# An encoder layer on one core: which queue issues the stores

## The chip, the cores and the metric

The kernel runs on one core of a Trainium2 chip. The metric is the time of one execution on the device in microseconds, without the host's work. Its engines each take their own instructions in the order in which they are written: TensorE (PE in the profile, PEld its weight loads), VectorE (DVE), ScalarE (ACT), GpSimd (POOL) and SyncE (SP). A DMA is issued by one of these queues: an issuing instruction waits until what it reads or overwrites is ready, and whatever stands behind it on the same queue waits too. The data is then moved by 16 DMA engines that all queues share.

## The reference

An encoder layer, applied to a sample of 1024 positions and to a prompt of 512, with the same weights and a width of 2048:

```
h = rms_norm(x, norm_g)
c_val, c_glu, c_gate, q, k, v, a_gate = split(h @ w_in)        # 2048 -> 5632, 44 blocks of 128
q, k = apply_rope(q), apply_rope(k)                            # 8 query heads, 2 key heads of 128
conv = silu(layer_norm(depthwise_conv31(c_val * sigmoid(c_glu)))) @ w_pw * silu(c_gate)
attn = banded_sink_attention(q, k, v, sink) * silu(a_gate)     # within 128 positions
y = rms_norm(x + concat(conv, attn) @ w_out, final_norm_g)
```

Everything is float32. The kernel splits each float32 operand of a large product into a high part, rounded for TensorE, and the low rest, and takes three products (high-high, high-low, low-high).

## The kernel before, in words

The positions lie along the free axis and 128 channels along the partitions. The sample comes first. Its input projection is cut into units of two column blocks and eight row blocks: a `Unit` computes a 2 by 2 block product with seven block products instead of eight (`P1` to `P7`), some 19 us on TensorE for each unit. It runs over the conv columns first (first half of the rows, then the second), then over gate, key, value, query and attention-gate columns. The first half's results are partial sums: `finish` (line 240) stores them into DRAM tiles named `part_...`. In the second half `finish` calls `add_into` (line 428), a DMA on GpSimd's queue that adds the stored part into the tile in SBUF; four or five products later the unit's `done` step works on the tile on VectorE and ScalarE and stores the result in DRAM (`gate_d`, `ag_d`, `h_d`, `q_d`, `k_d`, `v_d`).

For queries and keys the `done` step is `rotate` (line 947): `rope` (lines 928 to 933) makes two products on VectorE, and `put_rotated` (line 941) stores one of them and then adds the two halves of the other into the same DRAM rows with two `add_into` calls, which have to wait until the store has landed:

```
e.store(dst, o)
e.add_into(dst[0:half], b[half:])
e.add_into(dst[half:], b[0:half])
```

Behind the units come the prompt's projection, by whole columns (`Job`), then the pointwise product of the convolution, the output product of the sample (units again, with `y_d` and lines 1219 to 1239), and last the prompt's pointwise and output products (`last_run`). The convolution's taps run on VectorE beside all of these (line 906), fed from `h_d` and stored in `conv_d`; attention runs between the products of the prompt's jobs and reads `q_d`, `k_d`, `v_d` back and stores `att_d`. Weight blocks are loaded by SP into one of three `raw` buffers (lines 117 to 123, 332) and split by ScalarE and VectorE into one of three `hl` buffers (`parts`, lines 438 and 439). The low parts are stored once (`low_...`) and loaded for the prompt.

Tiles that are evicted from PSUM by line 217 come from two rings of four buffers, `g` and `u`; a buffer is free again when the store from it has landed. The products of `rotate` use a ring of four `a` buffers.

The order of work is written out by the program with lanes that give VectorE and ScalarE work between the products; then the tile framework puts each engine's instructions in an order by priorities and its own estimate of durations, and adds the waits.

Nearly all plain stores go through one helper, `store` (line 431). Accumulating DMAs go through `add_into`. The last rows of the prompt's output are stored by line 1531, which calls SP itself. All loads call SP themselves.

Of the kernel before, what the change touches and what calls it, by code (L numbers as in the profile page):

```python
# [358 lines left out]
class Encoder:  # L359
# [69 lines left out]
        self.nc.gpsimd.dma_start(dst, src, accum_op=ALU.add)  # L429

    def store(self, dst, src):
        self.nc.sync.dma_start(dst, src)

    def parts(self, hi, lo, x, g=None):

# [1421 lines left out]
```

## Time and profile before

| | |
|---|---|
| median of 3 runs | 2138.23 us |
| lowest and highest | 2134.34, 2139.43 us |
| span of the profiled execution | 2137.4 us |
| median against that span | 0.8 us more |
| TensorE busy | 2085.0 us, 98% |
| VectorE busy | 1668.7 us, 78% |
| ScalarE busy | 1063.8 us, 50% |
| GpSimd busy | 156.6 us, 7% |
| data moved by DMA | 473.04 MB, 221 GB/s on average |

The profile is of one execution. A line such as `L439 DVE ... hl<-raw,hl` names the line of the kernel, the engine, and what is written from what by the program's tile names. For a wait, the name behind `<-` is the instruction or DMA that ended it, as far as the semaphores tell; a wait for several things is put down to the last. Issuing a DMA isn't counted as busy time on SP, and it is on GpSimd.

### The profile page before, as it was taken

The numbers are of one execution on the slowest core, as the hardware profiler recorded it, in microseconds if no ns is written. First come the engines' busy times: TensorE is split into PE (matmuls) and PEld (weight loads), VectorE is DVE, ScalarE is ACT, GpSimd is POOL, SyncE is SP. The second block draws the span as 40 slices with busy tenths as digits, with TensorE's granted clock in tenths as the row PEclk, the third lists the DMA queues.
The fourth block names the chain that finished last, engine by engine and source line by source line (L and its number), as shares of the span: only waits on it lengthen the run. The fifth ranks groups of instructions, "written<-read, shape, count | busy, mean of one in ns | idle before, by whom it ended". The sixth has DMA issues, their size and how long they took to land. (4 is left out here: it accounts for less than half of the span.)

```text
span 2137.4 us, 26915 instructions
## 1 busy us (share of the span) xinstructions
PE 2085.0 (98%) x9330; PEld 1711.9 (80%) x9330; DVE 1668.7 (78%) x2551; ACT 1063.8 (50%) x1736; POOL 156.6 (7%) x184
## 2 busy tenths in 40 slices
PE   8999999999999999899999999999999989999998
PEld 7878888888888787688888888878888867887886
DVE  8757899988898788888887786668799667887543
ACT  7475436333554344554556776235545464563232
POOL 0001110000013233001000000000000001110000
PEclk9999999999999999999999999999999999999999
DMA  8888878854768888966664546886766369799952
GB/s 288 306 286 246 229 178 266 279 179 157 232 179 184 198 178 222 279 176 174 168 213 161 197 158 227 317 298 232 256 237 206 107 209 267 188 299 314 306 177 79
DMA packets 241209, 473.04 MB, mean 221 GB/s; under 512 B 23088, under 2 KB 80816, under 8 KB 241072
## 3 DMA queue, kind: packets, MB, share of 16 engines
q1 hardware_dynamic: 218992, 431.99, 60.5%
q0 software_dynamic: 22080, 39.33, 11.6%
q8 instruction: 73, 1.20, 0.2%
q14 instruction: 64, 0.52, 0.1%
HBM read 319.19 MB, written 152.04 MB: 220 GB/s over the span
## 5 line engine op out<-in xcount | busy, mean ns | idle before, releaser
L191 PE MATMUL a<-t,hl 128*128 128x512 f32 x2640 | 636.6, 392 | 22.5 <-ACT u L217 12.3
L191 PEld LDWEIGHTS a<-t,hl 128*128 128x128 f32 x2640 | 495.5, 189 | 132.8 <-ACT u L217 16.4
L438 ACT ACTIVATE hl<-raw 128x1024 fp32r<-128x1024 f32 (+1 forms) x330 | 296.2, 898 | 376.9 <-DVE raw L138 82.8
L439 DVE TENSOR_TENSOR hl<-raw,hl 128x1024 fp32r<-128x1024 f32 (+1 forms) x330 | 338.4, 1026 | 182.3 <-ACT hl L438 180.4
L906 DVE SCALAR_TENSOR_TENSOR f<-f,c_w_dw,f 128x1024 f32<-128x1024 f32 (+1 forms) x464 | 456.5, 1014 | 0.0
L578 PE MATMUL a<-t,hl 128*128 128x512 f32 x1344 | 328.9, 394 | 2.2 <-DVE f L848 2.2
L191 PE MATMUL c<-t,hl 128*128 128x512 f32 x1320 | 320.1, 390 | 1.6 <-ACT g L217 0.9
L578 PEld LDWEIGHTS a<-t,hl 128*128 128x128 f32 x1344 | 249.1, 188 | 53.0 <-DVE f L848 2.6
L191 PEld LDWEIGHTS c<-t,hl 128*128 128x128 f32 x1320 | 247.6, 188 | 53.8 <-ACT g L217 1.5
L578 PE MATMUL c<-t,hl 128*128 128x512 f32 x672 | 168.1, 397 | 0.0
L578 PE MATMUL b<-t,hl 128*128 128x512 f32 x672 | 162.6, 392 | 0.8 <-DVE hl L439 0.8
L191 PE MATMUL b<-t,hl 128*128 128x512 f32 x660 | 161.1, 390 | 0.0
L578 PEld LDWEIGHTS b<-t,hl 128*128 128x128 f32 x672 | 125.2, 188 | 26.1 <-DVE hl L439 1.2
L578 PEld LDWEIGHTS c<-t,hl 128*128 128x128 f32 x672 | 124.8, 189 | 24.4
L191 PEld LDWEIGHTS b<-t,hl 128*128 128x128 f32 x660 | 123.5, 188 | 25.1
L217 ACT ACTIVATE u<-a 128x512 f32<-128x512 f32 x114 | 67.2, 592 | 75.4 <-PE a L191 64.0
L217 ACT ACTIVATE g<-a 128x512 f32<-128x512 f32 x106 | 62.8, 592 | 76.8 <-PE a L191 70.3
L1540 PE MATMUL a<-hl,t 128*128 128x512 f32 x192 | 74.3, 390 | 0.0
L346 ACT ACTIVATE hl<-raw 128x1024 fp32r<-128x1024 f32 x44 | 46.4, 1054 | 46.7 <-PE b L578 15.2
L429 POOL DMA_DIRECT2D u<-part_out x16 | 14.0, 890 | 756.5 <-DVE t L439 697.4
L1044 ACT ACTIVATE p<-p,tiny 128x384 f32<-128x384 f32 (+1 forms) x96 | 54.5, 569 | 29.6 <-DVE tiny L1041 21.1
L438 ACT ACTIVATE a<-pt 128x512 fp32r<-128x512 f32 x64 | 38.0, 594 | 59.4 <-PE pt L1064 59.3
(312 smaller groups left out, 2581.2 us busy)
## 6 DMA issues: line engine op xcount, KB each, us to landing
raw<-w_in SPq DMA_DIRECT2D x171, 512.0 KB, 5.3
raw<-w_out SPq DMA_DIRECT2D x64, 256.0 KB, 4.5
raw<-w_out SPq DMA_DIRECT2D x31, 512.0 KB, 4.6
raw<-w_pw SPq DMA_DIRECT2D x24, 512.0 KB, 5.1
p<-xT_s SPq DMA_DIRECT2D x40, 256.0 KB, 5.3
f<-x_s SPq DMA_DIRECT2D x16, 512.0 KB, 7.2
f<-y_d SPq DMA_DIRECT2D x16, 512.0 KB, 5.9
y_s<-f SPq DMA_DIRECT2D x16, 512.0 KB, 4.6
```

Source lines behind the costliest of these rows:

```text
L191: nc.tensor.matmul(acc, hl[:, l, o, j, :], toks[j][:, r], start=name in FRESH and j == 0 and q == 0, stop=name in LAST and j == HALF - 1 a ...
L217: nc.scalar.activation(t, bank, AF.Copy)
L346: e.nc.scalar.activation(t[:, 0], raw, AF.Copy)
L429: self.nc.gpsimd.dma_start(dst, src, accum_op=ALU.add)
L438: nc.scalar.activation(hi, x, AF.Copy)
L439: nc.vector.tensor_tensor(lo, x, hi.bitcast(F32), ALU.subtract)
L578: nc.tensor.matmul(job.acc[0], hl[:, l, kk // HALF, kk % HALF, :], r, start=i == 0 and p == 0, stop=i == nk - 1 and p == 2,)
L906: nc.vector.scalar_tensor_tensor(t, h[:, j : j + T], w(j), t, ALU.mult, ALU.add)
L1044: nc.scalar.activation(p[:, 0:n], p[:, 0:n], AF.Exp, bias=nm[:, h : h + 1], accum_out=l[:, h : h + 1])
L1540: nc.tensor.matmul(acc, self.mix[self.KS[i]][:, m, b * P : (b + 1) * P], part[l].rearrange("p a b -> p (a b)"), start=i == 0 and p == 0, s ...
```

## The change

The helper `store` issues its DMA on GpSimd's queue and no longer on SP's. Nothing else in the program changes: `add_into`, the loads, and the prompt's last rows (line 1531) keep their queues.

```
     def add_into(self, dst, src):
         self.nc.gpsimd.dma_start(dst, src, accum_op=ALU.add)
 
     def store(self, dst, src):
-        self.nc.sync.dma_start(dst, src)
+        self.nc.gpsimd.dma_start(dst, src)
```

More of the change, by code (lines that the diff above doesn't have):

```diff
@@ L431, in store @@
     def store(self, dst, src):
-        self.nc.sync.dma_start(dst, src)
+        self.nc.gpsimd.dma_start(dst, src)
     def parts(self, hi, lo, x, g=None):
```

## The prediction

> **What bounds the kernel now.** I read the page first, then the busy time of each engine by stage, then who TensorE and VectorE wait for in the stage where GpSimd is used most, then the two DMA queues.
>
> ```profile
> span 2137.4 us, 26915 instructions
> PE 2085.0 (98%) x9330; PEld 1711.9 (80%) x9330; DVE 1668.7 (78%) x2551; ACT 1063.8 (50%) x1736; POOL 156.6 (7%) x184
> ```
>
> TensorE is busy 2085.0 of 2137.4 us, so all that any change can win is 52.4 us, and what a change can lose is whatever new waiting it forces on TensorE. SP and GpSimd matter only through that. By stage (busy us of each engine, clock, DMA share, GB/s):
>
> ```profile
> core 0: us, PE busy (x) PEld busy (x) DVE busy (x) ACT busy (x) POOL busy (x), PEclk, DMA share, GB/s
> ...
> 640.00:850.00 210.00, 203.04 (x895) 165.75 (x894) 168.02 (x226) 84.36 (x131) 69.08 (x80) 1.00 0.84 195
> 850.00:905.00 55.00, 44.68 (x188) 34.86 (x187) 44.16 (x65) 30.74 (x47) 8.45 (x10) 0.94 0.96 287
> 905.00:1400.00 495.00, 494.99 (x2308) 406.63 (x2307) 386.73 (x639) 275.68 (x466) 15.11 (x18) 1.00 0.64 200
> ...
> 1750.00:1910.00 160.00, 152.63 (x662) 123.81 (x661) 137.94 (x212) 95.38 (x154) 27.87 (x32) 0.99 0.88 244
> ```
>
> From 905 to 1400 us TensorE never stops. The place to look at is 640 to 850 us, where the ten key and query units of the sample sequence end: TensorE loses 7.0 us there, VectorE is idle for 210.0 - 168.0 = 42.0 us, and GpSimd issues 80 transfers. Who TensorE, and then VectorE, waits for in that window (us in total, times, longest):
>
> ```profile
> PE a L191 <- ACT u L217: 4.4, 3, 2.4
> PE a L191 <- DVE hl L439: 1.3, 1, 1.3
> PE a L191 <- ACT g L217: 1.2, 2, 0.7
> ```
>
> ```profile
> DVE a L932 <- issue: 17.8, 5, 8.0
> DVE a L932 <- DMA g<-part_kv: 7.1, 2, 6.7
> ...
> DVE u L882 <- DMA u<-part_gate: 3.2, 1, 3.2
> DVE a L932 <- DMA u<-part_q: 2.8, 2, 2.4
> DVE g L882 <- DMA g<-part_q: 2.4, 4, 1.2
> DVE a L932 <- DMA g<-part_q: 1.8, 1, 1.8
> DVE u L882 <- DMA u<-part_q: 1.7, 3, 0.7
> ```
>
> These seven groups hold 18 waits and 36.8 us, nearly all of VectorE's 42.0 us of idle time. Six name an accumulating DMA of line 429 (`add_into`, already on GpSimd's queue): the partial product is added into the tile and lines 932 and 882 need the sum. For the first the releaser isn't shown; line 932 needs the same sum and a free `a` tile, which another add of GpSimd's frees, so I count it in. VectorE takes its instructions in order, so a late add holds up the weight preparation of line 439 and, through ScalarE, TensorE.
>
> Why those adds are late is seen on the queues. Instructions of GpSimd, SP and VectorE from 740 to 750 us (start, us, what, idle before):
>
> ```profile
> 740.07 0.90 POOL L429 DMA_DIRECT2D g<-part_q  x1 [1.79 <-DVE g L237]
> 749.03 1.69 POOL L429 DMA_DIRECT2D q_d<-a  x2 [8.06 <-DVE a L932]
> 750.16 2.38 POOL L429 DMA_DIRECT2D u<-part_q  x2
> ```
>
> ```profile
> 742.23 0.32 SPq L432 DMA_DIRECT2D q_d<-u  x1
> ...
> 749.90 0.32 SPq L432 DMA_DIRECT2D q_d<-g  x1
> ```
>
> ```profile
> 747.97 0.69 DVE L932 TENSOR_TENSOR a<-g,f 128x512 f32<-128x512 f32 x1 [1.79 <-DMA g<-part_q]
> ```
>
> `put_rotated` stores the query (742.23, on SP) and then adds two halves into the same DRAM rows (749.03, on GpSimd). The adds must wait until the store has landed. GpSimd stands still for 8.06 us, and the next partial sums (750.16) stand behind.
>
> **The change part by part.** Every call of `store` moves: 464 issues (line 432's groups added up). The loads stay on SP, and the 16 stores of line 1531 too. Durations (ns, minimum/median/maximum) and landing times (us) of line 432 and of line 429, and who waits for a store:
>
> ```profile
> L432 SPq DMA_DIRECT2D att_d<-u x24: 525/561/922, 920.2 to 1733.5; - x24
> ...
> L432 SPq DMA_DIRECT2D q_d<-g x16: 319/320/566, 711.1 to 1048.4; - x16
> ...
> who waited for it (us, times):
>   POOL q_d L429: 75.4, 9
> ...
> DMA to landing us min/median/max: 2.0/3.8/11.7
> ```
>
> ```profile
> L429 POOL DMA_DIRECT2D q_d<-a x32: 821/848/1942, 693.1 to 849.5; - x32
> L429 POOL DMA_DIRECT2D u<-part_conv x16: 862/868/1005, 180.3 to 322.0; - x16
> ...
> DMA to landing us min/median/max: 2.8/6.0/11.9
> ```
>
> *Issue.* A store of 128 rows takes SP 320 ns; the nearest row on GpSimd, an add of 128 rows, takes 868 ns: 0.548 us more. GpSimd's busy time goes to 156.6 + 464 x 0.868 = 559 us, 26% of the span, so its sum is no bound; the order in it can be.
>
> *The rotated units (640 to 850 us).* Each add now has at least one store's issue ahead of it that ran beside it on SP. I charge each of the 18 VectorE waits 0.548 us: 9.9 us, and let all of it reach the end, since VectorE's idle time there is already made of such waits. The bounds: low, only the share of these waits that TensorE feels now (4.4 + 1.3 + 1.2 = 6.9 of 36.8, 0.19), 1.9 us; high, the store also lands later by the difference of the two medians, 6.0 - 3.8 = 2.2 us, so 18 x 2.75 = 49.5 us. I take 9.9, nearer the low end: the longer landing is that of an add, which reads what it adds to, and a store doesn't.
>
> *The queue behind.* A store waits for its data on GpSimd now, and adds and other stores wait behind it. Who holds SP in the same window (us, times, longest):
>
> ```profile
> SPq L123 <- DVE hl L439: 51.3, 10, 5.6
> SPq L432 <- DVE u L933: 44.9, 10, 9.4
> SPq L432 <- DVE g L933: 43.0, 10, 8.5
> ...
> SPq L1709 <- DMA q_d<-a: 9.5, 1, 9.5
> ```
>
> SP stands 87.9 us before the query stores, with gate stores and weight loads behind; this leaves SP, and is not new on GpSimd, which waits for the landing of those same stores anyway. What SP gains is loads that go out earlier. But its longest other wait (line 123) is for a buffer that VectorE frees, and stays.
>
> *Transition (850 to 905 us).* The one long stall of TensorE:
>
> ```profile
> PE a L191 <- ACT u L217: 5.3, 1, 5.3
> ```
>
> ScalarE is late because loads of the second sequence's rows (line 1709) wait for an `a` tile, freed by a query add (the 9.5 us above). The add stands behind a query store, so the store's later issue moves this by +0.5 us; bounds -5.3 (the load's cause gone) and +2.75.
>
> *Output units (1750 to 1910 us).* 32 stores into `y_d` join 32 adds. Each add can have one more issue ahead: at most 32 x 0.548 = 17.5 us for VectorE, which is idle 160.0 - 137.9 = 22.1 us there; I take 0. Without that cover it is +17.5; it could be a gain of all that TensorE loses there, 7.4 us.
>
> *Attention and the second sequence (905 to 1400 us).* The `att_d` stores have four pieces per row and take SP 561 ns. GpSimd's price lies between 868 ns (no more than for one piece) and 4 x 868 = 3472 ns; I take the lower end, since 64 rows cost 848 ns and 128 rows 868, so the count of pieces hardly shows. GpSimd is busy 15.1 of 495 us there and TensorE waits for nothing: 0. If one such store stood before a query add each time, 24 x 3.47 = 83 us would fall on a queue with 480 us free.
>
> *Freed loads.* What TensorE waits for after 905 us through ScalarE's preparation of loaded data:
>
> ```profile
> PE s L1030 <- ACT a L438: 3.5, 1, 3.5
> ...
> PE a L191 <- ACT hl L438: 2.3, 1, 2.3
> ...
> PE pt L191 <- ACT hl L438: 1.4, 1, 1.4
> ```
>
> Together 7.2 us. If stores no longer stand before those loads, between 0 and 7.2 us comes back. I take a third, -2.4 us: SP's loads also wait for one another's buffers.
>
> *Sum:* 9.9 + 0.5 + 0 + 0 - 2.4 = +8.0 us. The profiled span of 2137.4 becomes 2145.4; the median of the runs, 2138.2, stands 0.8 us above that span, so the forecast is 2146.2, slower by 0.37%. About 0.3% (6.4 us) is what a measurement of this kernel can tell from no change.
>
> A rule speaks against the change: the Trainium skill, SBUF — State Buffer, "SBUF: two separate sides", says that GpSimd, which builds its own descriptors, is shut out while VectorE runs in a two-port mode, so a transfer from GpSimd's queue can wait out VectorE's work. The trace bears little of it out: with VectorE busy most of each stage, the 16 adds of 180 to 322 us stay within 862 to 1005 ns. By the row the sum stays +8.0; by the rule it would be the fourth rival below.
>
> **The rivals.** *Faster.* SP no longer stands 87.9 us before query stores, gate stores free their tiles without passing weight loads, and adds aren't later because GpSimd was only waiting. Then some of the 7.0 us of 640 to 850, the 5.3 us at the transition and the 7.2 us of loads goes: 19.5 us, half of it gives 2128.5. It decides from the point where the store's later issue hides inside the 8.06 us. Against it: TensorE's waits name evictions and weights behind VectorE, not loads.
>
> *No difference.* VectorE's waits shift without growing, as TensorE feels only 0.19 of them: 18 x 0.548 x 0.19 + 0.5 - 2.4 = 0.0 us, so 2138.2. For it: TensorE's 98%.
>
> *GpSimd becomes the bound of the rotated units.* A unit takes 210/10 = 21.0 us. It has 8 adds (80 by ten) and now 4 stores: 12 x 0.868 = 10.4 us of issuing. Two landings of a query store are waited for; if both take 8.06 us with nothing else allowed past, the unit takes 26.5 us, 5.5 more, ten times: 55 us, 2193. It decides from a wait of (21.0 - 10.4)/2 = 5.3 us each, which lies between the medians 3.8 and 6.0. Against it: two stores' landings can overlap.
>
> *Starved issues.* VectorE's work holds up GpSimd's issues: all as long as the longest seen, 1942 ns. A rotated unit takes 12 x 1.942 + 8.06 = 31.4 us, 10.4 more, ten times: 104 us, 2242. Against it: the medians 848 and 868.
>
> That the stores don't move, or move without a new order on the engines, isn't a case I can price: the framework plans each engine's order anew, and a few us either way may come from that alone.
>
> **How the numbers follow.** Forecast 0.36, with a range of its own of 2141 to 2156; no difference 0.30; faster 0.22; GpSimd the bound 0.10; starved 0.02. The forecast's low end lies inside 0.3%, so 0.03 of it goes to "same": faster 0.22, same 0.33, slower 0.45. The range: 2127 takes in the faster case's middle and leaves 0.08 below; 2174 reaches two thirds of the way to the third rival's 2193 and leaves 0.10 above, starved issues among it.
>
> **What would show it.** Right: line 432 under GpSimd with some 868 ns each; VectorE's waits at lines 932 and 882 from 640 to 850 us above 36.8 us by about 10; the busy time of TensorE unchanged and its idle time there up from 7.0 to about 17 us; the stage 905 to 1400 still full. Wrong: waits at 932 and 882 that stay or shrink (no difference, or faster), SP's waits for line 933 gone and TensorE's idle time after 850 us smaller (faster), GpSimd busy or waiting for all of the stage and the units at 24 us or more (the bound), issues well over 1 us while VectorE runs (starved). A loss in a stage that I priced at 0, above all 905 to 1400 us or 1750 to 1910 us, would make the prediction wrong even if the total fits.

## The result, and the profile after

| | before | after |
|---|---|---|
| median (4 runs each, side by side) | 2138.83 us | 2164.01 us |
| lowest and highest | 2134.34, 2141.11 us | 2161.74, 2165.36 us |
| ratio, 95% interval | | 1.011 [1.0093, 1.0126] |
| span of the profiled execution | 2137.4 us | 2163.3 us |

The change makes the kernel about 25 us slower. The two profiled executions differ by 25.9 us, and TensorE alone accounts for it. The page of the kernel after, its span and the busy time of each engine:

```profile
span 2163.3 us, 27145 instructions
PE 2096.7 (97%) x9330; PEld 1719.8 (79%) x9330; DVE 1666.9 (77%) x2551; ACT 1062.4 (49%) x1736; POOL 416.2 (19%) x648
```

The same 9330 matmuls kept TensorE busy for 2096.7 us instead of 2085.0: +11.7 us for the same work, which is a matter of the clock. Its idle time went from 2137.4 - 2085.0 = 52.4 to 2163.3 - 2096.7 = 66.6 us: +14.2. The two add up to 25.9. VectorE and ScalarE did the same work in the same time. GpSimd's busy time rose by 259.6 us to 19% of the span, so that sum isn't the bound.

Where the idle time lies is seen by stage. First the stages of the kernel before that the prediction didn't show, then those of the kernel after (us from the start; length, then busy us of each engine, clock, DMA share, GB/s):

```profile
0.00:160.00 160.00, 150.06 (x646) 122.53 (x647) 113.26 (x186) 100.25 (x163) 0.20 (x4) 1.00 0.85 294
...
1400.00:1560.00 160.00, 156.50 (x714) 129.85 (x713) 124.31 (x212) 84.33 (x143) 0.00 (x0) 0.99 0.74 252
1560.00:1750.00 190.00, 186.69 (x853) 152.65 (x852) 147.50 (x256) 96.45 (x179) 0.00 (x0) 1.00 0.55 186
...
1910.00:2137.00 227.00, 216.40 (x960) 178.38 (x958) 120.25 (x202) 68.65 (x109) 0.00 (x0) 0.99 0.70 227
```

```profile
0.00:160.00 160.00, 149.52 (x638) 121.73 (x639) 110.98 (x183) 98.18 (x160) 33.32 (x65) 0.99 0.82 290
...
640.00:850.00 210.00, 202.08 (x889) 165.99 (x888) 167.56 (x223) 84.72 (x130) 94.47 (x124) 0.99 0.84 191
850.00:905.00 55.00, 45.11 (x183) 35.74 (x181) 41.68 (x55) 31.61 (x46) 13.00 (x18) 0.91 0.97 299
905.00:1400.00 495.00, 488.45 (x2265) 400.16 (x2265) 392.58 (x653) 274.88 (x469) 64.90 (x101) 0.99 0.65 207
1400.00:1560.00 160.00, 159.47 (x733) 132.23 (x732) 113.05 (x190) 77.84 (x124) 15.74 (x28) 1.00 0.68 227
1560.00:1750.00 190.00, 182.51 (x833) 149.02 (x832) 146.84 (x262) 92.94 (x181) 30.28 (x55) 1.00 0.50 169
1750.00:1910.00 160.00, 152.09 (x657) 123.50 (x656) 133.79 (x207) 96.66 (x158) 40.60 (x58) 0.98 0.86 242
1910.00:2163.00 253.00, 237.69 (x1031) 194.98 (x1029) 134.81 (x225) 78.11 (x124) 15.74 (x27) 0.97 0.67 224
```

| stage | TensorE idle before | after | difference |
|---|---|---|---|
| 0 to 160 us, first units | 9.9 | 10.5 | +0.5 |
| 640 to 850, rotated units | 7.0 | 7.9 | +1.0 |
| 850 to 905, transition | 10.3 | 9.9 | -0.4 |
| 905 to 1400, attention, prompt | 0.0 | 6.5 | +6.5 |
| 1400 to 1560 | 3.5 | 0.5 | -3.0 |
| 1560 to 1750 | 3.3 | 7.5 | +4.2 |
| 1750 to 1910, output units | 7.4 | 7.9 | +0.5 |
| 1910 to the end | 10.6 | 15.3 | +4.7 |

From 160 to 640 us the idle time is 0.0 us before and 0.2 after. The stretches are cut at fixed times, and the work lies some us later in the kernel after, so a stall at an edge can change sides. Even so the picture is plain: the rotated units, where I expected the loss, hold little of it. It lies in three places: near 1350 us, at 1600 to 1640 and near 1960. Compared at the same count of matmuls, the kernel after is behind by 5.4 us at 1340 us of the kernel before, by 10.5 at 1450, 11.0 at 1600, 15.1 at 1615, 16.2 at 1910 and 26.0 at the end, so these places hold some 19 of the 26 us, the slower clock included.

The +11.7 us of busy time belong to the stalls. One of them, in the windows view of the kernel after:

```profile
1956.50:1959.90 3.40, 0.00 (x0) 0.00 (x0) 3.23 (x12) 2.32 (x3) 0.00 (x0) 0.99 0.95 293
1959.90:1970.10 10.20, 9.66 (x26) 7.62 (x27) 6.50 (x26) 1.32 (x3) 0.00 (x0) 0.50 0.79 242
1970.10:1980.30 10.20, 10.20 (x46) 8.17 (x45) 6.02 (x7) 3.88 (x5) 0.54 (x1) 1.00 0.66 208
```

TensorE stands still for 3.4 us, and for the 10.2 us after that the granted clock is 0.50: 26 matmuls instead of 46. So the stall is paid twice. In the trace of the kernel before the clock is at 0.50 for 13.7 us ahead of the last matmul, in three places; after, for 41.0 us in seven, each a multiple of 3.41 us long. Half of the 27.3 us between them is 13.7 us, about the 11.7 us seen. The Trainium skill, TensorE: Matmul & The Clock Gate, "Part 1: The HAM clock gate (the "warmup" mystery)", says that the clock is halved after an idle window of some 3.4 us and that the window runs freely. The trace agrees with the length of the window. On the idle time it differs, since shorter stalls halved the clock too: 2.98 us, up to 895 us in the kernel after, and 2.43 us at 1808 us in the kernel before.

What a store costs on GpSimd, and when its data lands (line 432, the kernel after; ns minimum/median/maximum, us):

```profile
L432 POOL DMA_DIRECT2D att_d<-u x24: 717/726/1402, 925.6 to 1749.2; - x24
...
L432 POOL DMA_DIRECT2D q_d<-g x16: 539/578/1469, 709.7 to 1054.3; - x16
...
L432 POOL DMA_DIRECT2D y_d<-g x16: 539/568/578, 1784.4 to 1939.3; - x16
...
  POOL q_d L429: 99.3, 24
  ACT u L217: 25.5, 7
...
DMA to landing us min/median/max: 2.3/5.2/10.0
```

The issue takes some 0.54 to 0.58 us, not the 0.868 us of an accumulating DMA; against SP's 0.32 us the difference is 0.22 to 0.26 us. The data lands 5.2 us after the issue where it was 3.8. ScalarE's evictions into `u` tiles (line 217) now wait 25.5 us in all for stores to land, where it was 8.1. The landing isn't later for every kind: for `y_d` the median is 6.5 us after and 6.6 before.

### The profile page after: what moved, and what is told of

Same layout as the page of the kernel before. It is cut to its first block, busy times and chain, and to the rows that moved or that the text cites. A ratio compares the mean times of both kernels' runs of the same rounds, so it can differ in the third digit from the quotient of the medians.

```text
span 2163.3 us, 27145 instructions
## 1 busy us (share of the span) xinstructions
PE 2096.7 (97%) x9330; PEld 1719.8 (79%) x9330; DVE 1666.9 (77%) x2551; ACT 1062.4 (49%) x1736; POOL 416.2 (19%) x648
## 4 chain that ended last, share of the span: by engine, by line
PE 67%; issue 12%; DMA 10%; DVE 5%; POOL 3%; ACT 2%; SPq 0%; ACTq 0%; POOLq 0%; DVEq 0%
PE a L191 18%; PE a L578 11%; PE c L191 9%; PE c L578 5%; PE b L578 5%; PE b L191 4%; PE s L1540 2%; PE pv L1059 2%; PE s L1030 2%; PE s L191 2%; DMA a<-ag_d 1%; PE pt L1064 1%; DVE hl L439 1%; PE a L1540 1%; PE pv L1540 1%
## 5 line engine op out<-in xcount | busy, mean ns | idle before, releaser
L191 PE MATMUL a<-t,hl 128*128 128x512 f32 x2640 | 639.0, 393 | 26.6 <-ACT u L217 18.0
L191 PE MATMUL c<-t,hl 128*128 128x512 f32 x1320 | 322.3, 392 | 6.7 <-ACT u L217 5.8
L191 PEld LDWEIGHTS c<-t,hl 128*128 128x128 f32 x1320 | 248.7, 189 | 59.8 <-ACT u L217 6.7
L578 PE MATMUL c<-t,hl 128*128 128x512 f32 x672 | 172.5, 405 | 5.1 <-DVE hl L439 4.0
L578 PEld LDWEIGHTS c<-t,hl 128*128 128x128 f32 x672 | 128.5, 195 | 31.5 <-DVE hl L439 4.4
L346 ACT ACTIVATE hl<-raw 128x1024 fp32r<-128x1024 f32 x44 | 46.4, 1054 | 49.5 <-DMA raw<-w_in 26.6
L439 DVE TENSOR_TENSOR a<-pt,a 128x512 fp32r<-128x512 f32 x64 | 43.9, 686 | 29.4 <-ACT a L438 29.0
```

What stands on the lines that cost most here:

```text
L191: nc.tensor.matmul(acc, hl[:, l, o, j, :], toks[j][:, r], start=name in FRESH and j == 0 and q == 0, stop=name in LAST and j == HALF - 1 a ...
L346: e.nc.scalar.activation(t[:, 0], raw, AF.Copy)
L439: nc.vector.tensor_tensor(lo, x, hi.bitcast(F32), ALU.subtract)
L578: nc.tensor.matmul(job.acc[0], hl[:, l, kk // HALF, kk % HALF, :], r, start=i == 0 and p == 0, stop=i == nk - 1 and p == 2,)
```

## The experiments

In all but two of them the helper takes the kind of the store, and a list names the kinds that go to GpSimd's queue; only that list differs:

```
 def store(self, dst, src, kind):
-    self.nc.sync.dma_start(dst, src)
+    (self.nc.gpsimd if kind in ON_GPSIMD else self.nc.sync).dma_start(dst, src)
```

The framework plans each engine's order anew from this. Some kernels get the order of before on TensorE, VectorE and ScalarE, and others don't; that is said where it matters. SP's other 751 DMAs, nearly all of them loads, are put in order anew as well, and the traces show where. With the rotated stores alone, each of them stands where it stood. In the run of five kinds 7 stand elsewhere (1476 to 1533 us), with the output units' stores alone 45 (all from 1777 us on), and in the kernel after 142. Those 142 lie, among others, at 45 to 138, 1311 to 1476, 1568 to 1606 and 1912 to 2041 us of the kernel before, so each of the three places of the loss has loads in a new order in it or just ahead of it. The kernel before ran beside each: its medians there were 2140.1 to 2143.5 us, single runs 2133 to 2147.

### The early stages alone, the late ones alone

```
+ON_GPSIMD = ("low", "part", "sums", "xr", "h", "gate", "rot", "v")
```

> The stores of the sample's projection and everything before it (partial sums, low parts, block sums, h_d, gates, rotated, v_d, xr_d) move to GpSimd, those behind stay on SP. By the trace after, which had gained 7.0 us at the start of the prompt's jobs: +4 to +7 us, 2142 to 2145. If the loss behind 900 us only follows from stores that come earlier: the whole +25 us, 2164.

Measured: 2144.9 us, ratio 1.0028 [1.0013, 1.0043], which fits the +4 to +7 us. These are the stores of the sample's units.

```
+ON_GPSIMD = ("part_out", "h2", "conv", "gate2", "att", "msum", "mix", "y", "out", "cs", "mix2")
```

> The other stores (the prompt's gates and h_d, conv_d, att_d, cs, mix_d, block sums of mix_d, partial sums of the output units, y_d, y_s) move, those of the sample's projection stay on SP. By the trace after: +18 to +21 us, 2156 to 2159, with the stalls near 1350, 1620 and 1960 us. If the effects of both halves don't add up (the order that the framework plans decides, not the queue): anything from 2138 to 2164 and stalls in other places.

Measured: 2154.16 us, ratio 1.0066 [1.0043, 1.009]. That is some 14 us, less than the 18 to 21 expected. So about two thirds of the loss come from stores of the attention, the prompt and the output product, in stages that the prediction priced at 0 or had no term for. The two parts, 0.28% and 0.66%, give 0.94%, which lies within the interval of the whole change.

### The rotated units

```
+ON_GPSIMD = ("rot", )
```

> Only the 26 stores of put_rotated move to GpSimd; TensorE's, VectorE's and ScalarE's instructions keep the order of before. The prediction's step (each of 18 waits of VectorE from 640 to 850 us grows by 0.548 us and all of it reaches the end) gives +9.9 us, 2148. The theory formed from the trace after (that stage gained only 2.5 us with all stores moved; the loss lies in stalls of the later stages) gives 0 to +3 us, 2138 to 2142. If GpSimd were the bound of the rotated units: 2160 or more.

Measured: 2142.91 us, ratio 1.0012 [0.9998, 1.0026]: +2.6 us, not to be told from nothing. It was 30 stores (24 of `q_d`, 6 of `k_d`), not 26. The order on the three engines is that of before, and SP's loads keep theirs.

```
+ON_GPSIMD = ("xr", "h", "rot", "v", "mix2")
```

> The stores of xr_d, h_d of the sample, query and key, v_d and the sample's mix_d (from the pointwise product) move to GpSimd: the kinds that leave the order of TensorE, VectorE and ScalarE as it was. The queue alone is changed. Theory: only the rotated stores cost, as when they moved alone (0.1%): +1 to +4 us, 2141 to 2144. Rival, any store on GpSimd costs by its later landing: +5 us or more.

Measured: 2147.38 us, ratio 1.0028 [1.0016, 1.0041]: +6.0 us (3.4 to 8.8), on the rival's side, though the interval reaches into the theory's. The order on TensorE, VectorE and ScalarE is that of before here too, and so is SP's but for 7 loads, where the kernel falls no further behind. So this loss belongs to the queue alone. Who GpSimd waits for in 640 to 850 us, in the kernel before and in this one (us, times, longest):

```profile
POOL q_d L429 <- DMA q_d<-u: 4.8, 3, 3.4
...
POOL q_d L429 <- DMA q_d<-g: 3.0, 2, 2.4
...
POOL k_d L429 <- DMA k_d<-g: 0.5, 1, 0.5
```

```profile
POOL q_d L429 <- DMA q_d<-u: 28.0, 8, 7.0
...
POOL q_d L429 <- DMA q_d<-g: 19.5, 7, 5.2
...
POOL k_d L429 <- DMA k_d<-g: 6.5, 2, 4.5
```

GpSimd's time behind the landing of a stored query or key goes from 8.3 to 54.0 us in these three groups, since the add stands right behind its store on the same queue. The later partial sums wait behind it, as predicted, but VectorE's waits at lines 932 and 882, of which these are the two largest groups, don't grow in all, and those for the weights do:

```profile
DVE a L932 <- DMA u<-part_q: 17.1, 4, 7.5
DVE a L932 <- DMA g<-part_q: 10.2, 4, 4.3
DVE hl L439 <- ACT hl L438: 7.9, 5, 2.2
```

All groups at 932 and 882 make 33.1 us where it was 37.7 (36.8 in the prediction's seven); 17.8 us of that earlier sum had no releaser shown. Line 439's wait for ScalarE was 3.3 us and is 7.9. TensorE does lose something here: it is idle for 10.3 us after 7.0, its waits for ScalarE's evictions are 9.0 us after 5.6, and one stretch of 3.41 us at half clock is new. By which path the late adds reach it isn't shown.

### The output units

```
+ON_GPSIMD = ("y", "out")
```

> Only the stores into y_d and y_s move to GpSimd; TensorE keeps its order, VectorE's differs in 75 lines of the listing. Theory: the stall near 1950 us (8 us with the clock's loss) comes from y_d's stores, whose landing frees the g tiles that SP's gate loads wait for at the head of its queue: +6 to +9 us, 2146 to 2149, with the stall there. Rival, the stall comes from what the other late stores shift: 0 to +2 us.

Measured: 2153.4 us, ratio 1.0058 [1.0038, 1.0078]: +12 us, half of the whole loss, from 48 stores (`y_d` and `y_s`). TensorE keeps the order of before, but VectorE's differs at 36 instructions and SP's at 45, in the stretch of the stall too. The chain is seen in the instructions of this kernel (start, us, what, idle before), SP first, then GpSimd, VectorE and TensorE:

```profile
1923.99 5.33 SPq L1382 DMA_DIRECT2D g<-gate_d  x2
...
1930.32 0.42 SPq L1423 DMA_DIRECT2D a<-ag_d  x1
```

```profile
1923.76 0.55 POOL L432 DMA_DIRECT2D y_d<-g  x1 [7.03 <-DVE g L1226]
```

```profile
1937.38 0.69 DVE L1431 TENSOR_TENSOR a<-a 128x512 f32<-128x512 f32 x1 [5.14 <-DMA a<-ag_d]
1945.10 0.86 DVE L645 TENSOR_SCALAR f<-c_ident,tinyr 128x128 fp32r<-128x128 f32 x4
```

```profile
1946.02 1.58 PE L650 MATMUL s<-f,ones_r 128*128 128x512 f32 x2 [4.36 <-DVE f L645]
```

The store of 1923.76 holds a `g` tile. The gate load of line 1382 needs that tile and stands at the head of SP until the store has landed, to 1929; the loads of `ag_d` behind it go out later (1930.32), VectorE waits 5.14 us for one, and the statistics behind it (lines 611 to 645) reach TensorE 4.36 us late. In the kernel before, the load went out 3.6 us earlier and VectorE had nearly nothing to wait for (SP, VectorE):

```profile
1921.97 0.32 SPq L432 DMA_DIRECT2D y_d<-g  x1
...
1926.77 0.32 SPq L1423 DMA_DIRECT2D a<-ag_d  x1
1927.82 0.32 SPq L1382 DMA_DIRECT2D g<-gate_d  x1
```

```profile
1932.65 0.69 DVE L1431 TENSOR_TENSOR a<-a 128x512 f32<-128x512 f32 x1 [0.25 <-DMA a<-ag_d]
```

The store takes no longer to land: 5.5 us there (1921.97 to 1927.45) and 5.2 us here (1923.76 to 1928.94). It goes out 1.8 us later, since VectorE makes its data 1.4 us later, with a product of line 1431 now ahead. What differs most is the order on SP. Before, the load of `ag_d` (1926.77) stands ahead of the gate load that needs the landing (1927.82), which waits only 0.4 us. Here the gate load stands ahead of it, and waits 4.6 us.

The kernel after shows the same chain in its waits from 1910 us on, SP's and then TensorE's:

```profile
SPq L1382 <- DMA y_d<-g: 12.0, 3, 5.2
```

```profile
PE s L650 <- DVE f L645: 4.1, 1, 4.1
```

The counterpart leaves only these two kinds on SP and moves all the others:

```
+ON_GPSIMD = (every kind but "y" and "out")
```

> All stores of the change on GpSimd's queue except the two of the output units (y_d, y_s, lines 1238 and 1239, and the rows of the result behind them), which stay on SP. Theory, the loss is a sum of separate places, each with its own store: the stall near 1950 us goes, and with it the 0.58% of the run where those stores alone were moved; the stalls near 106, 1350 and 1620 us stay: a ratio of 1.004 to 1.007 (2149 to 2155). Rival, a queue that is loaded all through the kernel, or the new order of the engines, is the cause wherever it shows: the ratio stays at 1.009 or more.

Measured: 2150.62 us, ratio 1.0036 [1.0023, 1.005], slightly below the theory's 1.004 to 1.007 and far from the rival's 1.009. Of the wait for line 645 there is this left, in the same stretch of this kernel:

```profile
PE s L650 <- DVE f L645: 0.3, 1, 0.3
```

With these 48 stores on GpSimd's queue the stall comes, and without them it goes, so they are its source. How much of it is the queue and how much the order that SP and VectorE get along with it isn't shown: the two changed together, and in this kernel SP's order in that stretch is the one of before.

### The stall near 1350 us

Here a block of weights lands late, while attention's last products (line 1163, eight of them, one for each head) share VectorE with the weight preparation. Six runs looked for what is behind it.

```
+ON_GPSIMD = ("att", )
```

> Only the 24 att_d stores move. Theory: SP's load of att_d (line 1158) stands at the head of SP's queue until the store on the other queue has landed, 7 to 9 us, with a weight load behind it, and TensorE stalls near 1340 to 1350 us: +5 to +8 us, 2145 to 2148. Rival, the stall needs the other stores of that stage (cs, mix_d, block sums) gone from SP: 0 to +2 us and no wait of line 1158 over 3 us.

Measured: 2141.73 us, ratio 1.0003 [0.9989, 1.0017]; no stall there. The theory on `att_d` alone falls. TensorE's order differs from before's at 41 matmuls here and SP's at 29 loads, so a new order by itself need cost nothing.

```
+ON_GPSIMD = ("part_out", "h2", "conv", "gate2", "cs")
```

> Only the stores of the prompt's partial results, the prompt's h rows, the convolution's rows, the prompt's gates and the low parts of the convolution (conv_d, h_d, part_out and the like) on GpSimd's queue. This looks for the store behind the stall of TensorE near 1350 us, where a block of weights landed late. Theory, it is one of these stores: a stall of 3 to 5 us between 1335 and 1365 us and a step of about +8 us there, ratio 1.003 to 1.005. Rival, it needs several kinds of stores together, or is the attention's sums: no stall over 2 us there, ratio up to 1.0015.

Measured: 2142.7 us, ratio 1.0003 [0.999, 1.0016], with a stall of 2.3 us at 1355. Neither answer as it was put: the stall is there, small, and costs nothing in the end.

```
+ON_GPSIMD = ("msum", "mix")
```

> Only the stores of the two second-half sums (msum_S and the like) and of the sample's mixed attention rows (xT) on GpSimd's queue. Theory, the two stalls of TensorE at 1605 to 1635 us come from these stores, whose landing frees the tile that ScalarE's eviction waits for: two stalls of 1.5 to 3 us there, a step of +4 to +5, ratio 1.001 to 1.003. Rival, they come with other stores queued ahead: no stall over 1 us there, ratio within 1.001. A stall near 1350 us would say that the block of weights that is late there hangs on these stores.

Measured: 2150.58 us, ratio 1.0041 [1.0026, 1.0056]. The two stalls at 1605 to 1635 us that this run was made for came out at 0.9 and 0.7 us, so the rival holds there: these stores alone aren't enough. But the place near 1350 us is in trouble. TensorE, VectorE and the transfers from 1320 to 1400 us, and how many of the eight products of line 1163 fall into 1340 to 1400, in the kernel before, with the sums and mixed rows alone (first view only), and after:

```profile
1320.00:1400.00 80.00, 80.00 (x355) 66.28 (x354) 50.85 (x71) 25.91 (x30) 0.00 (x0) 1.00 0.90 315
```

```profile
L1163 DVE TENSOR_TENSOR a<-a,a 128x1024 f32<-128x1024 f32 x4 | 4.9, 1227 | 13.2 <-DMA a<-ag_d 13.2
```

```profile
1320.00:1400.00 80.00, 74.40 (x306) 59.87 (x305) 52.45 (x73) 26.05 (x31) 10.36 (x19) 0.94 0.95 350
```

```profile
1320.00:1400.00 80.00, 73.86 (x312) 59.99 (x311) 54.93 (x75) 27.91 (x35) 15.15 (x28) 0.96 0.99 367
```

```profile
L1163 DVE TENSOR_TENSOR a<-a,a 128x1024 f32<-128x1024 f32 x6 | 7.3, 1221 | 5.6 <-DMA a<-ag_d 5.6
```

In the kernel before the transfers run at 315 GB/s with 4 heads in the stretch, and TensorE never stops. After, they run at 367 GB/s with 6 heads, the 16 DMA engines are full (0.99), and TensorE is idle for 6.1 us; from 1400 to 1500 us the rate then is 212 GB/s where it was 263. The same data is fetched earlier and meets the weights. This goes together in every run: the six kernels with 4 or 5 heads there (before, `att_d` alone, the rotated units alone, the early stages, the output units, the five kinds in the old order) have 312 to 320 GB/s and lose 0 to 0.2 us from 1320 to 1400, and the eight with 5 or 6 heads and at least 335 GB/s lose 2.3 to 6.6.

What lets the heads run ahead? The first theory was SP's pace: before, SP issues a mixed row 4 to 12 us after it is made, because weight loads stand ahead of it, and its tile is free for the next head only then.

```
+ON_GPSIMD = (every kind but "y", "out", "msum" and "mix")
```

> As the run that kept the output units' stores on SP, and the stores of the attention's mixed rows and sums (mix_d, msum) are kept on SP too; the other stores are on GpSimd's queue, and the order on TensorE is the one of that run. Before, SP issues each mixed row 4 to 12 us after VectorE has made it (made at 1325.6 and 1333 us, issued at 1336.3 and 1340.1), because weight loads stand ahead; the row's buffer comes free late, and the next heads' loads and products are spread out: the 8 products of line 1163 lie from 1324 to 1414 us. With these stores on GpSimd they lie from 1327 to 1400 us and take VectorE's time from the weights. Theory, that pacing by SP is what was lost: with it back, the stalls near 1350 us and at 1615 to 1630 us go, and the ratio falls from 1.0036 to within 0.9985 to 1.0015. Rival, the new order of the engines alone runs the heads ahead (they were compressed, to 1396 us, in the run of the prompt's other stores too): a stall of 2 to 5 us stays between 1340 and 1365 us, and the ratio is 1.002 to 1.004.

Measured: 2148.01 us, ratio 1.0039 [1.0025, 1.0053], the same as with `msum` and `mix` moved. The theory falls: the heads lay from 1327 to 1401 us as without this edit, and a stall of 2.2 us stayed at 1361, which is the rival's answer. TensorE's order is that of the run with every kind but `y` and `out` moved, and the heads run ahead with it though these stores are back on SP. The profiled execution of this kernel was its fastest (2141.99 us, 6 us below the median), so its trace can't show where the others lost the rest.

Two more kernels tried the theory that the loads run ahead because SP no longer waits for the data of the stores. The first is the changed kernel with a store of 16 numbers on SP from the same tile behind each store (extra work, 464 small transfers):

```
     def store(self, dst, src):
         self.nc.gpsimd.dma_start(dst, src)
+        self.nc.sync.dma_start(<a new DRAM tile of 16 numbers>, <16 numbers of src>)
```

> As the changed kernel, and behind every store SP issues a store of 16 numbers from the same tile into a scratch row, so that SP stops for the same data as before, and the loads behind it go out no earlier. Theory that SP's loads run ahead and crowd out the weight blocks (raw tiles landing 7.9 us median and 15.2 longest from 1300 to 1400 us, against 6.2 and 10.1 before): the median goes back to 6 to 6.5 us there, the stall near 1350 us goes, and the time falls to 2145 to 2155. Rival, lateness on GpSimd's side or the planned order: stays at 2160 to 2170, the 464 small transfers costing little or a few us.

Measured: 2164.0 us, ratio 1.0104 [1.0074, 1.0135]: nothing restored. The stall at 1356 us was smaller (2.2 us), the others were there. This kernel has 464 transfers more, and TensorE's order differs from the changed kernel's at 18 matmuls, so the run speaks against the theory without excluding it.

The second is the changed kernel with the loads of lines 1158, 1159 and 1351 on GpSimd's queue, where they can't hold up the weights on SP:

```
-nc.sync.dma_start(f, seq.att_d[h // GROUP][:, h % GROUP, :])
-nc.sync.dma_start(g, seq.ag_d[h])
+nc.gpsimd.dma_start(f, seq.att_d[h // GROUP][:, h % GROUP, :])
+nc.gpsimd.dma_start(g, seq.ag_d[h])
...
-e.nc.sync.dma_start(held[-1], self.cs_d[i])
+e.nc.gpsimd.dma_start(held[-1], self.cs_d[i])
```

> As the changed kernel, with the loads of att_d and ag_d (lines 1158 and 1159) and of cs (line 1351) on GpSimd's queue too, behind the stores that they wait for. TensorE's order is that of the changed kernel, VectorE's differs in 32 lines from it. Theory (these loads hold up SP's weight loads): the stall near 1350 us goes, 8 us less than the changed kernel, 2154 to 2158. Rival (the order in which the framework puts TensorE's, VectorE's and ScalarE's work): the stall stays, 2162 to 2166.

Measured: 2164.9 us, ratio 1.0091 [1.0073, 1.0109]; a stall of 4.4 us stayed at 1360. Neither run bears its theory out.

What the traces of all these kernels do show is the planned order. In the six that lose nothing here, the last of the eight loads of `att_d` (line 1158) stands behind 171 weight loads on SP's queue. In the eight that lose, it stands behind 164 to 168, or is on GpSimd's queue (the last run). So the heads run ahead where the framework has put their loads earlier.

So near 1350 us it is shown that attention's loads come earlier and bunch with the weights whenever TensorE loses there. How the loss splits between the new order and the queue stays open: no run had the heads' new order without moved stores, and none had all the stores of this stage moved with the order of before.

No kernel here was faster than the one before.

## Why the prediction was right, and where its steps were wrong

The direction and the whole range held: 2164.0 us lies in 2127 to 2174. The forecast of 2146.2 was a third of the loss, its own range of 2141 to 2156 missed the time, and the reason was largely another one. That the range held is in part luck: it reached to 2174 for the sake of the third rival, GpSimd as the bound, which didn't come. The prediction also left the new order on the engines out of its sum, as "a few us either way". The three places with some 19 of the 26 us all have SP's loads in a new order, and where the order stayed, the most that was measured is 6.0 us (76 of the 464 stores). By its steps:

- *Issue, 0.548 us more.* Wrong in size. The price of an accumulating DMA isn't that of a plain store: 0.54 to 0.58 us on GpSimd against 0.32 on SP. GpSimd's busy time was 416.2 us, not 559. For `att_d`, with four pieces a row, I bounded the issue by 0.868 to 3.47 us; it took 0.726, less than either.
- *Rotated units, +9.9 us.* Wrong in size and in the link to VectorE. The forecast was 18 waits at lines 932 and 882 going from 36.8 us to about 47, and TensorE's idle time from 7.0 to 17. The waits at these lines, 37.7 us with the two smallest groups, went to 27.3 us, and the idle time to 7.9. Nor are the ten units of this stage all rotated: one of keys and four of queries are, with 12 adds each, and the others are of values and attention gates, with 4. The kernel after, the three longest waits of VectorE in 640 to 850 us:

```profile
DVE a L932 <- DMA u<-part_q: 15.4, 5, 6.4
DVE hl L439 <- ACT hl L438: 10.2, 6, 3.2
DVE a L932 <- DMA g<-part_q: 8.4, 4, 5.8
```

  The first part of the mechanism is there: GpSimd stands behind the landing of its own stores, 57.6 us instead of 8.3 in the same three groups (26.6, 23.1 and 7.9). What it cost in time is 2.6 us (-0.4 to 5.6) for the rotated stores alone, and 6.0 us (3.4 to 8.8) for the five kinds whose move left the order as it was; the low bound, 1.9 us, was nearer than the 9.9 I took.
- *Transition, +0.5 us.* Right: TensorE's idle time there is 9.9 us after 10.3. The long stall stayed (6.9 us at 870); its clock fell a little further, 0.91 after 0.94.
- *Output units, 0.* This failed most. I looked for adds held up by an issue, within the units, and named VectorE's idle time as the cover. The stage itself is as it was (+0.5 us). The loss came behind it: a load that needs the tile of such a store stops SP until the store has landed, and what now stands behind that load is late for TensorE. The landing took no longer; the load's place on SP was new. This alone was 12 us; the bound of 17.5 us would have held it, for another reason.
- *Attention and second sequence, 0.* Wrong: 6.5 us of idle time in a stage that was full, where the transfers of the heads were pulled forward onto the weights. My bounds were on GpSimd's issuing; the DMA engines' share, 0.64 over 495 us, hid 0.90 in the 80 us that counted.
- *1560 to 1750 us.* I had no term for it. It lost 4.2 us. TensorE waits for ScalarE's evictions (4.5 us in two stalls, after 0.7), and these wait longer for tiles whose stores have to land. The rows of before and after in 1590 to 1640 us:

```profile
ACT u L217 <- DMA msum_S<-u: 6.3, 1, 6.3
```

```profile
ACT u L217 <- DMA msum_S<-u: 9.6, 1, 9.6
...
ACT g L217 <- DMA part_out<-g: 2.2, 1, 2.2
...
ACT u L217 <- DMA part_out<-u: 2.0, 1, 2.0
```

  Such a wait alone isn't enough: with `msum` and `mix` moved it is 8.4 us, and the two stalls stay under 1 us. The cause of this place is open.
- *Freed loads, -2.4 us.* Right in sign and size: the 3.5 us wait at line 1030 is gone, and 1400 to 1560 us gains 3.0. That the loads did it isn't shown. In the kernel after TensorE's order is new from 1407 to 1452 us, with attention's products earlier, and in the runs that kept TensorE's order a stall of 2.3 to 3.2 us stays there.
- *No term for the clock.* All nine stalls of 2.8 us or more in the two traces go with 3.4 to 10.2 us at half clock, and one of the five of 2.3 to 2.5 us does. It is 11.7 of the 25.9 us, and with the idle time of the three places it makes up most of what the sum of 8.0 lacked.

Of the rivals, "faster" and "no difference" are out by the interval. GpSimd wasn't the bound: the rotated units didn't grow, 889 matmuls after 895 in the same 210 us. Starved issues would have been well over 1 us; the medians of the stores are 0.54 to 0.73, with VectorE busy for 84% of 1750 to 1910 us while `y_d` was stored at 0.57. The adds of `part_q` did rise well over 1 us in the median (1.47 and 1.49, after 1.12 and 0.97). The Trainium skill's rule in SBUF — State Buffer, "SBUF: two separate sides", shows no sign of having decided here. It isn't tested either, since no view tells which of VectorE's operations ran in the two-port mode that it speaks of.

## What to carry to other kernels

A store's cost isn't its issue alone: follow each stored tile to whoever needs its buffer next, an eviction or a load at the head of another queue, look at what stands behind that one, and price the chain in every stage, also where an engine's average shows room. A stall of TensorE of some 3 us costs nearly as much again through the clock (11.7 us of it beside 14.2 of idle time here), so a few short stalls outweigh many small delays. And when some DMAs change their queue, the framework can put those that stay in a new order: compare the order of the loads too before a difference is put down to the queue, and look for bunched transfers in the DMA share over stretches of tens of us, not over a stage.

## What the runs showed of the hardware

- A plain store of 128 rows takes GpSimd 0.54 us to issue, an accumulating DMA of the same size 0.87 us (`part_conv`, 16 each).
- The adds of the partial sums `part_q` got dearer where the rotated stores share their queue. Before and after (ns):

```profile
L429 POOL DMA_DIRECT2D u<-part_q x16: 862/974/1708, 674.2 to 829.6; - x16
```

```profile
L429 POOL DMA_DIRECT2D u<-part_q x16: 847/1490/1781, 678.4 to 834.0; - x16
```

  The median rose by 0.52 us, and by 0.47 with the 30 rotated stores alone. The adds of `part_conv` and `part_out` stayed at 0.87 though stores share their queue too. Whether it is the work ahead on the queue or a port shared with VectorE wasn't tried.
- The clock falls to 0.50 in pieces of 3.41 us after a stall, up to three in a row (10.2 us after a stall of 4.1).
